# A hybrid mLSTM / RWKV-7 / mixture-of-experts layer on one core: RWKV rows a chunk ahead, output norms as fused pairs, two down pieces behind the product's halves

## Chip, core and metric

The kernel runs on one core of a Trainium2 chip. The metric is the device time of one execution in microseconds (us). The engines are TensorE (PE, with its weight loads PEld), VectorE (DVE), ScalarE (ACT), GpSimd (POOL) and SyncE (SP, which here only issues DMAs).

## What is computed

One layer over 256 context and 2048 latent tokens of width 1024, batch 1, all in float32. Cut to what the change touches:

```python
def _modulate(z, shift, scale):
    return _layernorm(z) * (1 + scale) + shift

    mixed = _mixer(_modulate(ctx, sh1c, sc1c), _modulate(x, sh1, sc1), ...)
    x = _layernorm(ALPHA * x + g1 * (mixed[:, CTX_LEN:] @ w_out[l]), ln1_g[l], ln1_b[l])
    ffn = _hier_moe(_modulate(x, sh2, sc2), ...)
    x = _layernorm(ALPHA * x + g2 * ffn, ln2_g[l], ln2_b[l])

    # in the mixer, RWKV-7, per head, forwards and backwards
    def step(state, inp):
        r_t, w_t, k_t, v_t, kh_t, a_t = inp
        removed = jnp.einsum('zhvk,zhk->zhv', state, kh_t)
        state = (state * w_t[:, :, None, :] - removed[..., None] * (kh_t * a_t)[:, :, None, :]
                 + v_t[..., None] * k_t[:, :, None, :])
        return state, jnp.einsum('zhvk,zhk->zhv', state, r_t)

    # in the experts, 32 of them, top 2 of one group for each token
    hb = jax.nn.silu(xb @ ex_gate[e]) * (xb @ ex_up[e])
    return (hb @ ex_down[e]) * w[:, None]
```

The mixer projects the modulated input, convolves it, runs an mLSTM group and an RWKV-7 group of eight heads each, in both directions, and joins them.

## The kernel before, in words

Stages run one after the other: the input's transpose `make_hT` with the modulation (0 to 125 us), input projection and convolution, token tiles, the mLSTM, RWKV (1241 to 1978 us), the output projection with its two norms (1978 to 2355 us), the experts (2355 to 3520 us) and the last norm. Matrix products that need float32 precision take each operand as a rounded part H and a rest L and add three products, so every operand is split: a cast on ACT or VectorE gives H, a subtraction on VectorE gives L. A scheduler with a model of times sets the order on every engine, except in RWKV, where the program's own order stands for TensorE, VectorE, ACT and SP.

**First stage** (lines 198 to 219). Tokens come in chunks of up to 512. GpSimd issues the loads of four tiles x (line 205), VectorE takes their statistics (lines 75 to 79, the root on ACT) and normalises (line 207). TensorE transposes (line 213), ACT modulates into `hval` (215), VectorE casts to H (218) and subtracts for L (219). The pool of x has five buffers.

**RWKV.** There are nine groups of 256 tokens, each of four chunks of 64, handled for both directions at once (36 chunks). A group needs four builds (two halves, two directions). A build loads `pk` (SP, line 891), takes exponentials (`exps`, ACT, 907 to 909), forms the rows KR and BK (`rows`, VectorE, 919 to 923), multiplies them on TensorE (`products`, 929) with a mask on VectorE into GM (933), and transposes BK into BT (`turn`, 938, 939). A solve inverts a group's triangular matrices by 31 pairs of VectorE operations (`steps`, 978 and 980) on a matrix sM that comes from GM over DRAM; `back` writes the result to DRAM and again into GM, and `join` (1007 to 1024) completes it on TensorE. A chunk itself is a chain between TensorE and ACT or VectorE: start and keys (1051 to 1067), inverse (1076, 1079), update (1086), state (VectorE, 1092 and 1094), outputs (1102, 1105). The next chunk starts from the state S. The main loop (1123 on) calls the chain's parts and puts the builds, the solve's steps and the joins of other groups between them; `PLAN` says which builds belong to which chunk, `CUT` how far the solve has come.

**Output projection** (`project`, from line 1293). For sixteen tiles of 128 tokens: the product on TensorE, the residual on VectorE (1306), then two layer norms in `norm_sums` (1190 to 1201): the mean from sums that earlier passes accumulate, ACT squares (1197) and takes the root (1198), VectorE the reciprocal, and an ACT Identity pass (1201) scales. After it come the gain (1310, VectorE), the bias (1312), the second norm's scale (1315) and shift (1316); 1312 and 1315 run on GpSimd for the first fourteen tiles, on VectorE for the last two. TensorE then transposes the result for the router (1329).

**Experts** (`moe`). Every expert has at least one block of 128 tokens; more blocks run under branches (lines 1710 to 1716). The three weight matrices come through a ring of raw buffers `eraw` and are split into twelve pieces by `split` (1513 cast on ACT, 1514 subtraction on VectorE): 0 to 3 gate, 4 to 7 up, 8 to 11 down. `gate_up` multiplies gate, takes Silu on ACT, multiplies up in two halves of 256 columns; `mult(h)` (1594, VectorE) multiplies a half into `act`, which TensorE transposes (1522) and which is split again (aH 1530, aL 1535) for the down product `epo` in `tail`. `add` scales the output (1623) and adds it to memory.

## Time and profile before

| | us |
|---|---|
| three runs | 3574.02, 3576.32, 3585.05 (median 3576.32) |
| the profiled execution, own time | 3583.68 |
| its span | 3582.1 |
| busy TensorE / weight loads | 2910.9 / 2442.9 |
| busy VectorE / ACT / GpSimd | 2360.3 / 1389.8 / 880.8 |

The mean granted clock of TensorE in it is 0.878 of full speed, and 602.62 MB were moved by DMA, a mean of 168 GB/s. Busy shares over the span (81%, 66%, 39%, 25%) are means over stages with different limits, so the stages have to be looked at one by one. "Idle before, releaser" in a row says how long an engine stood idle just before the instruction, and which event ended that.

### The profile page before, as it was taken

The page shows a single profiled execution, that of the slowest core. Times are in us where ns is not written, and L with a number is a line of the kernel's source. Part 1 is how long each engine was busy: PE and PEld are TensorE (multiplying, and loading weights), DVE is VectorE, ACT ScalarE, POOL GpSimd, SP SyncE. Part 2 cuts the span into 40 slices and gives each one's busy share as a digit, 9 for nine tenths or more (in the row PEclk, how much of TensorE's full clock was granted, in tenths as well). Part 3 has the DMA queues.
Part 4 walks back from the last instruction along what each step waited for, and adds up shares of the span by engine and source line. Part 5 has one row for each costly group of instructions (what it writes and reads, how often), then busy time and mean ns, then how long its engine had stood idle before and what let it go on. Part 6 is the DMA issues. An engine that isn't in the chain of part 4 may idle for free. (4 is left out here: it accounts for less than half of the span.)

```text
span 3582.1 us, 61557 instructions
## 1 busy us (share of the span) xinstructions
PE 2910.9 (81%) x24042; PEld 2442.9 (68%) x24042; DVE 2360.3 (66%) x3863; ACT 1389.8 (39%) x2197; POOL 880.8 (25%) x874
## 2 busy tenths in 40 slices
PE   7999999999889735776666688958888888988892
PEld 4788778987677625665656466757777777877772
DVE  6788888666878745556663677766757545566437
ACT  3432232255453313333333244444535434344223
POOL 1000000024555600111112656531221221221100
PEclk9999999999878756887878799869999999999996
DMA  5333331354685345666663544277978747586535
GB/s 201 119 110 100 120 106 61 104 171 174 203 240 156 119 92 135 148 165 158 154 153 101 177 144 133 93 260 228 314 243 271 254 127 257 161 282 215 175 107 200
DMA packets 471690, 602.62 MB, mean 168 GB/s; under 512 B 127221, under 2 KB 312337, under 8 KB 471313
## 3 DMA queue, kind: packets, MB, share of 16 engines
q1 hardware_dynamic: 413617, 441.15, 39.0%
q0 software_dynamic: 36736, 129.33, 12.9%
q10 hardware_dynamic: 20960, 27.20, 2.3%
q8 instruction: 225, 3.69, 0.4%
q14 instruction: 152, 1.25, 0.1%
HBM read 453.24 MB, written 144.33 MB: 167 GB/s over the span
## 5 line engine op out<-in xcount | busy, mean ns | idle before, releaser
L1514 DVE TENSOR_TENSOR eL<-eraw,eH 128x1024 fp32r<-128x1024 f32 x384 | 443.9, 1218 | 22.1 <-ACT eH L1513 22.1
L329 DVE SCALAR_TENSOR_TENSOR cacc<-P,cw,cacc 128x1008 f32<-128x1008 f32 (+3 forms) x320 | 398.7, 1247 | 54.5 <-ACT cacc L304 44.0
L1513 ACT CAST eH<-eraw 128x1024 fp32r<-128x1024 f32 x384 | 367.8, 1054 | 1.4 <-DVE eL L1514 1.4
L929 PE MATMUL rpg<-KR,BK 64*128 64x128 f32 (+1 forms) x1152 | 121.0, 369 | 211.3 <-DVE KR L923 182.5
L929 PEld LDWEIGHTS rpg<-KR,BK 64*128 64x128 f32 x1152 | 105.0, 267 | 226.7 <-issue 180.5
L263 PE MATMUL in_ps<-hH,w_H 128*128 128x512 f32 (+1 forms) x664 | 251.1, 380 | 1.3 <-ACT pl_ev L355 1.3
L263 PE MATMUL in_ps<-hL,w_H 128*128 128x512 f32 (+1 forms) x664 | 250.2, 377 | 1.0 <-DVE hL L219 1.0
L263 PE MATMUL in_ps<-hH,w_L 128*128 128x512 f32 (+1 forms) x664 | 248.2, 374 | 0.0
L1547 PE MATMUL epo<-eH,aH 128*128 128x512 f32 x408 | 182.3, 447 | 40.0 <-PEq L1710 31.3
L933 DVE TENSOR_TENSOR GM<-rpg,rmask 128x512 f32<-128x512 f32 (+1 forms) x144 | 88.4, 656 | 154.5 <-PE rpg L929 152.3
L1624 POOL DMA_INDIRECT ACC<-yo,ids x32 | 136.7, 4270 | 201.6 <-DVE yo L1623 195.6
L1547 PE MATMUL epo<-eL,aH 128*128 128x512 f32 x408 | 170.2, 417 | 0.0
L1547 PE MATMUL epo<-eH,aL 128*128 128x512 f32 x408 | 163.1, 412 | 0.0
L1564 POOL DMA_INDIRECT xg<-H,ids x48 | 57.6, 1200 | 392.4 <-PE ept L1522 277.6
L1530 ACT CAST aH<-ept 128x256 fp32r<-128x256 f32 x102 | 38.2, 375 | 289.8 <-PE ept L1522 289.8
L1547 PE MATMUL epu<-eL,xH 128*128 128x256 f32 x512 | 148.7, 296 | 0.0
L263 PEld LDWEIGHTS in_ps<-hH,w_H 128*128 128x128 f32 x664 | 125.2, 190 | 34.0 <-issue 10.3
L237 POOL DMA_DIRECT2D w_raw<-in_w_in x28 | 21.2, 757 | 513.4 <-DVE w_L L251 368.9
L1547 PE MATMUL epu<-eH,xL 128*128 128x256 f32 x512 | 146.7, 292 | 0.0
L298 ACT COPY P<-in_ps 128x512 f32<-128x512 f32 (+1 forms) x92 | 51.4, 558 | 239.8 <-PE in_ps L263 239.8
L263 PEld LDWEIGHTS in_ps<-hL,w_H 128*128 128x128 f32 x664 | 125.9, 190 | 24.1 <-issue 2.1
L1547 PE MATMUL epu<-eH,xH 128*128 128x256 f32 x512 | 141.6, 296 | 0.0
(474 smaller groups left out, 8367.0 us busy)
## 6 DMA issues: line engine op xcount, KB each, us to landing
eraw<-in_ex_gate SPq DMA_DIRECT2D x64, 1024.0 KB
eraw<-in_ex_up SPq DMA_DIRECT2D x64, 1024.0 KB
eraw<-in_ex_down SPq DMA_DIRECT2D x64, 1024.0 KB
pk<-PK SPq DMA_DIRECT2D x144, 320.0 KB
PK<-pk POOLq DMA_DIRECT2D x36, 768.0 KB
ada_w<-in_w_ada SPq DMA_DIRECT2D x32, 512.0 KB
v<-MV SPq DMA_DIRECT2D x50, 264.0 KB
kc<-KTd SPq DMA_DIRECT2D x50, 256.0 KB
```

The costliest lines, as they stand in the source:

```text
L237: self.wld = nc.gpsimd.dma_start(w[:, 4:8, o:o + cn], src[:, 4:8])
L263: nc.tensor.matmul(o, a[:, k, :], b, start=i == 0, stop=i == 3 * KT - 1)
L298: nc.scalar.copy(P[:, t0:t0 + n], ps)
L329: nc.vector.scalar_tensor_tensor(o, img[:, r0 + sy:r1 + sy, c0 + sx:c1 + sx], wt(dy, dx), o, op0=OP.mult, op1=OP.add)
L929: nc.tensor.matmul(pG[e][:, q, b.cols], b.BK[HD[e], c, q, :], b.KR[HD[e], c, q, b.cols], start=True, stop=True, tile_position=(64 * e, 0))
L933: nc.vector.tensor_tensor(b.GM[:, c, e::2, b.cols], pG[e][:, :, b.cols], m, op=OP.mult)
L1513: self.cp = nc.scalar.copy(H, w)
L1514: nc.vector.tensor_tensor(L, w, H, op=OP.subtract)
L1530: self.lastc = nc.scalar.copy(A[0][:, ks], ps[:, :step])
L1547: self.pe = nc.tensor.matmul(o, a[:, k, :], b[:, kw, c], start=first and i == 0, stop=last and i == 2)
L1564: return nc.gpsimd.indirect_dma_start(out=x, out_offset=None, in_=self.H2, in_offset=bass.IndirectOffsetOnAxis(ap=ids, axis=0))
L1624: nc.gpsimd.indirect_dma_start(out=self.ACC, out_offset=bass.IndirectOffsetOnAxis(ap=cur[:, 0:1], axis=0), in_=y, in_offset=None, compute_ ...
```

## The change

1. In the first stage, the normalisation of all chunks but the first goes from VectorE to GpSimd, and every second cast to H from VectorE to ACT.
2. In RWKV, all eight builds of the first two groups are made ahead of the first join, each loaded two ahead; in the main loop exponentials and rows of a build come one chunk ahead of its products, loads are issued earlier still, and the solve's steps are cut anew. GM and BT are now allotted with the products; the pool of WC has six buffers.
3. `norm_sums` no longer writes the normalised tile: the two multiply-and-add pairs that follow take mean and reciprocal as per-row operands, two fused VectorE passes for each norm, and the pass over the bias yields the sum for the second norm.
4. In `gate_up` only ten of the twelve pieces are split ahead; the last two behind `mult(0)`. `mult(1)` moves from `tail` to the end of `gate_up`, and two pieces of the next expert are no longer bound behind the last split of this one.

```diff
-                    nc.vector.tensor_scalar(x, x, mu, rs, op0=OP.subtract, op1=OP.mult)
+                    (nc.vector if ci == 0 else nc.gpsimd).tensor_scalar(x, x, mu, rs, op0=OP.subtract, op1=OP.mult)
...
-                    nc.vector.tensor_copy(H, val[:, :n])
+                    (nc.scalar.copy if k % 2 else nc.vector.tensor_copy)(H, val[:, :n])
...
-            CUT = {1: (24, 17), 2: (15, 9), 3: (1, 1)}
+            CUT = [(32, 27, 24), (23, 17, 15), (13, 9, 8), (1, 1, 1)]
...
+                todo = [(n, c2, d) for n in range(2) for c2 in range(2) for d in range(2)]
+                bs = [Build(*a) for a in todo[:2]]
+                for b in bs:
+                    b.exps()
+                    b.rows()
+                for i in range(8):
+                    b = bs[i]
+                    if i + 2 < 8:
+                        bs.append(Build(*todo[i + 2]))
+                    b.products(0)
+                    b.turn(0)
+                    if i + 2 < 8:
+                        bs[i + 2].exps()
+                    b.products(1)
+                    b.turn(1)
+                    if i + 2 < 8:
+                        bs[i + 2].rows()
+                    if i == 3:
+                        old = Solve(0)
...
+                for i in range(36):
+                    n, cc = i // 4, i % 4
+                    k, work, ready = nxt, ready, []
...
+                    if first:
+                        for b in work:
+                            b.products(0)
+                            b.products(1)
+                        if n and n < 8:
+                            z = Solve(n + 1)
+                        old.join(0)
+                    k.start()
+                    k.keys()
+                    if z:
+                        z.steps(CUT[cc][0])
+                        if cc == 3:
+                            z.back()
+                    k.query()
+
+                    more, loads = (loads[:len(plan(i + 1))], loads[len(plan(i + 1)):])
+                    if more:
+                        more[0].exps()
+                    if first:
+                        for b in work[:1]:
+                            b.turn(0)
+                    else:
+                        for b in work:
+                            b.products(0)
+                    if more:
+                        more[0].rows()
+                    k.inverse()
+                    if more[1:]:
+                        more[1].exps()
+                        more[1].rows()
+                    ready = more
...
+                    if z:
+                        z.steps(CUT[cc][1])
+                    k.update()
+                    k.state()
+                    k.outputs()
...
+                    if first:
+                        old.join(1)
+                    if z:
+                        z.steps(CUT[cc][2])
...
-        nc.vector.tensor_tensor(nm, nmu, rs, op=OP.mult)
-        nc.scalar.activation(out, x, AF.Identity, bias=nm, scale=rs)
+        return nmu, rs
...
-                self.norm_sums(tp, x, (sm[:, 0:1], sm[:, 1:2]), "o1", x, t2)
-                nc.vector.scalar_tensor_tensor(x, x, 1.0, l1g, op0=OP.mult, op1=OP.mult, accum_out=sm[:, 2:3])
-                tail = nc.vector if m >= 14 else nc.gpsimd
-                tail.tensor_tensor(x, x, l1b, op=OP.add)
+                nmu, rs = self.norm_sums(tp, x, (sm[:, 0:1], sm[:, 1:2]), "o1", t2)
+                nc.vector.scalar_tensor_tensor(x, x, nmu, l1g, op0=OP.add, op1=OP.mult)
+                nc.vector.scalar_tensor_tensor(x, x, rs, l1b, op0=OP.mult, op1=OP.add, accum_out=sm[:, 2:3])
                 nc.scalar.dma_start(self.ACC[r0], x)
-                self.norm_sums(tp, x, (sm[:, 2:3], sb), "o2", t2, t2, eps2)
-                tail.tensor_tensor(t2, t2, sc2, op=OP.mult)
-                nc.vector.tensor_tensor(t2, t2, sh2, op=OP.add)
+                nmu, rs = self.norm_sums(tp, x, (sm[:, 2:3],), "o2", t2, eps2)
+                nc.vector.scalar_tensor_tensor(t2, x, nmu, sc2, op0=OP.add, op1=OP.mult)
+                nc.vector.scalar_tensor_tensor(t2, t2, rs, sh2, op0=OP.mult, op1=OP.add)
...
+                def more(n, behind):
+                    if R:
+                        with tc.issue_after(behind.ins):
+                            for _ in range(n):
+                                W.append(split(R, len(W)))
...
-                mult(0)
+                m = mult(0)
+                more(2, m)
...
+                mult(1)
...
-                W += [split(Rs[e], i) for i in range(len(W), 12)]
+                W += [split(Rs[e], i) for i in range(len(W), 10)]
...
+                    W = [split(Rs[e + 1], i) for i in range(2)]
                     with tc.issue_after(self.evac[0]), tc.issue_after(self.evac[1]):
-                        W = [split(Rs[e + 1], i) for i in range(AHEAD)]
+                        W += [split(Rs[e + 1], i) for i in range(2, AHEAD)]
```

VectorE, in RWKV where one group's fourth chunk ends and the next group's first chunk runs (S is the state, KR and BK the rows of two builds, GM their masked products, sT and sY a solve's steps); before:

```order
L1094 TENSOR_TENSOR S<-ts,WC 128x512
L919 TENSOR_TENSOR KR_14802<-pk,E_10872 128x4x2x64
L920 TENSOR_TENSOR BK<-pk 128x4x2x64
L921 TENSOR_TENSOR BK<-pk 128x4x2x64
L923 TENSOR_TENSOR KR_14802<-pk,E_10872 128x4x2x64
L919 TENSOR_TENSOR KR_14810<-pk,E_10873 128x4x2x64
L920 TENSOR_TENSOR BK<-pk 128x4x2x64
L921 TENSOR_TENSOR BK<-pk 128x4x2x64
L923 TENSOR_TENSOR KR_14810<-pk,E_10873 128x4x2x64
L933 TENSOR_TENSOR GM_14804<-rpg,rmask 128x4x128 x4
L933 TENSOR_TENSOR GM_14812<-rpg,rmask 128x4x128 x4
L1092 TENSOR_TENSOR ts<-S,rzK 128x512
```

The same place in the changed kernel:

```order
L921 TENSOR_TENSOR KR_14739<-pk,E_10873 128x4x2x64
L935 TENSOR_TENSOR GM_14698<-rpg,rmask 128x4x128 x2
L1087 TENSOR_TENSOR ts<-S,rzK 128x512
L1089 TENSOR_TENSOR S<-ts,WC 128x512
L935 TENSOR_TENSOR GM_14814<-rpg,rmask 128x4x128 x4
L935 TENSOR_TENSOR GM_14840<-rpg,rmask 128x4x128 x4
L973 TENSOR_TENSOR sT<-sM,sY 128x31
L975 TENSOR_TENSOR sY<-sY,sT 128x31
L973 TENSOR_TENSOR sT<-sM,sY 128x60
```

The rows of both builds now end ahead of the fourth chunk's state, and behind the masks stand the first steps of the next solve (five pairs of them, then the chunk's own state update).

VectorE, from the end of one expert to the second half of the next one's product (xL the next tokens' split, aL that of act, ne the branch's count, eL weight pieces, yo the output of the expert before); before:

```order
L1535 TENSOR_TENSOR aL<-ept,aH 128x256
L1661 COPY ne<-blk 1x1
L1662 TENSOR_LOAD ne
L1664 COMPARE_AND_BRANCH
L1664 UNCONDITIONAL_BRANCH x2
L1514 TENSOR_TENSOR eL<-eraw,eH 128x1024 x2
L1623 SCALAR_TENSOR_TENSOR yo<-epo,ids,g2b 128x512
L1514 TENSOR_TENSOR eL<-eraw,eH 128x1024
L1623 SCALAR_TENSOR_TENSOR yo<-epo,ids,g2b 128x512
L1514 TENSOR_TENSOR eL<-eraw,eH 128x1024 x9
L1594 TENSOR_TENSOR act<-act,epu_35414 128x256
L1535 TENSOR_TENSOR aL<-ept,aH 128x256
```

The same place in the changed kernel, from the piece ahead of xL on:

```order
L1532 TENSOR_TENSOR eL<-eraw,eH 128x1024
L1553 TENSOR_TENSOR xL<-epx,xH 128x512 x2
L1553 TENSOR_TENSOR aL<-ept,aH 128x256
L1688 COPY ne<-blk 1x1
L1532 TENSOR_TENSOR eL<-eraw,eH 128x1024
L1689 TENSOR_LOAD ne
L1691 COMPARE_AND_BRANCH
L1691 UNCONDITIONAL_BRANCH x2
L1532 TENSOR_TENSOR eL<-eraw,eH 128x1024 x3
L1650 SCALAR_TENSOR_TENSOR yo<-epo,ids,g2b 128x512
L1532 TENSOR_TENSOR eL<-eraw,eH 128x1024
L1650 SCALAR_TENSOR_TENSOR yo<-epo,ids,g2b 128x512
```

It goes on there with the last three pieces ahead of act, and what follows:

```order
L1532 TENSOR_TENSOR eL<-eraw,eH 128x1024 x3
L1622 TENSOR_TENSOR act<-act,epu_35348 128x256
L1532 TENSOR_TENSOR eL<-eraw,eH 128x1024 x3
L1553 TENSOR_TENSOR aL<-ept,aH 128x256
L1622 TENSOR_TENSOR act<-act,epu_35349 128x256
```

Before, twelve pieces stand ahead of act's first half; now one stands ahead of xL, eight between the count and the first half, and three between that half and aL.

## Rows read from the trace of the kernel before

**Rows 1.** Windows: length, busy PE, PEld, DVE, ACT, POOL, clock, DMA share, GB/s.

```profile
1241.00:1378.00 137.00, 56.78 (x626) 48.36 (x628) 57.18 (x123) 26.54 (x47) 15.72 (x20) 0.54 0.40 96
1378.00:1949.00 571.00, 383.53 (x9082) 340.10 (x9074) 346.86 (x785) 211.52 (x368) 102.61 (x196) 0.79 0.59 149
...
2355.00:3520.00 1165.00, 999.03 (x5516) 871.01 (x5516) 664.59 (x881) 487.93 (x641) 235.29 (x111) 0.92 0.68 216
```

**Rows 2.** Waits of PE, 1452 to 1892 us: total, times, longest.

```profile
PE rpg L929 <- DVE KR L923: 99.9, 18, 6.1
```

**Rows 3.** Timeline of PE: start, duration, engine, line, operation, idle before.

```profile
1713.29 2.08 PE L929 MATMUL rpg<-KR,BK 64*128 64x128 f32 x16 [5.20 <-DVE KR L923]
```

**Rows 4.** Timeline of DVE in RWKV.

```profile
1307.75 1.29 DVE L933 TENSOR_TENSOR GM<-rpg,rmask 128x512 f32<-128x512 f32 x2 [1.72 <-PE rpg L929]
1308.96 0.20 DVE L978 TENSOR_TENSOR sT<-sM,sY 128x31 f32<-128x31 f32 x1
...
1332.10 0.19 DVE L980 TENSOR_TENSOR sY<-sY,sT 128x31 f32<-128x31 f32 x1
1352.33 0.69 DVE L919 TENSOR_TENSOR KR<-pk,E 128x512 f32<-128x512 f32 x1 [20.04 <-ACT E L907]
...
1377.55 0.69 DVE L1094 TENSOR_TENSOR S<-ts,WC 128x512 f32<-128x512 f32 x1
...
1891.77 0.69 DVE L1094 TENSOR_TENSOR S<-ts,WC 128x512 f32<-128x512 f32 x1
...
1948.97 0.69 DVE L1094 TENSOR_TENSOR S<-ts,WC 128x512 f32<-128x512 f32 x1
```

**Rows 5.** Waits of PE in the experts, 2376 to 3393 us.

```profile
PE ept L1522 <- DVE act L1594: 82.4, 29, 3.0
```

**Rows 6.** Timeline of DVE in one expert.

```profile
2700.45 10.30 DVE L1514 TENSOR_TENSOR eL<-eraw,eH 128x1024 fp32r<-128x1024 f32 x9
2710.67 0.41 DVE L1594 TENSOR_TENSOR act<-act,epu 128x256 f32<-128x256 f32 x1
2712.27 0.43 DVE L1535 TENSOR_TENSOR aL<-ept,aH 128x256 fp32r<-128x256 f32 x1 [1.19 <-ACT aH L1530]
```

**Rows 7.** Timeline of PE in the same expert.

```profile
2711.14 0.69 PE L1522 MATMUL ept<-ident,act 128*128 128x128 f32 x2 [2.95 <-DVE act L1594]
...
2714.87 0.40 PE L1547 MATMUL epo<-eH,aL 128*128 128x512 f32 x1
```

**Rows 8.** Windows in the experts.

```profile
2711.10:2714.40 3.30, 2.90 (x13) 2.53 (x14) 0.68 (x2) 0.78 (x2) 0.00 (x0) 0.51 1.05 422
2714.40:2718.00 3.60, 3.60 (x19) 3.04 (x20) 1.82 (x5) 1.76 (x4) 1.00 (x1) 1.00 1.01 392
...
2588.00:2612.00 24.00, 20.76 (x113) 17.85 (x112) 18.35 (x23) 14.41 (x19) 13.88 (x3) 0.93 1.01 358
```

**Rows 9.** Timeline of POOL in the first stage.

```profile
80.37 2.13 POOL L205 DMA_DIRECT2D x<-in_x  x4 [18.15 <-PE hps L213]
100.74 1.61 POOL L205 DMA_DIRECT2D x<-in_x  x3 [18.24 <-PE hps L213]
```

**Rows 10.** Lines 207, 1238 and 812: count, ns min/median/max, first and last start.

```profile
L207 DVE TENSOR_SCALAR x<-x,hx_mv x18: 758/811/815, 19.6 to 111.1; 128x1024 f32<-128x1024 f32 x18
...
L1238 POOL TENSOR_SCALAR ln_g<-ln_g x1: 2796/2796/2796, 1986.5 to 1986.5; 128x1024 f32<-128x1024 f32 x1
...
L812 POOL TENSOR_SCALAR pk<-pk,cv,kb x36: 548/555/2603, 725.2 to 994.5; 128x256 f32<-128x256 f32 x36
```

**Rows 11.** Timeline of DVE in the first stage.

```profile
92.99 0.81 DVE L207 TENSOR_SCALAR x<-x,hx_mv 128x1024 f32<-128x1024 f32 x1
```

**Rows 12.** Waits of DVE, 1241 to 1978 us.

```profile
DVE sT L978 <- DMA sM<-BL: 54.8, 8, 7.9
```

**Rows 13.** Lines 1201, 1312 and 1315 in the output projection.

```profile
L1201 ACT ACTIVATE x<-x,o_ns x16: 1227/1242/1246, 2050.8 to 2332.7; 128x1024 f32<-128x1024 f32 x16
...
L1312 POOL TENSOR_TENSOR x<-x,ln_b x14: 2339/2390/3372, 2056.2 to 2305.8; 128x1024 f32<-128x1024 f32 x14
...
L1315 POOL TENSOR_TENSOR t<-t,sc2b x14: 2349/2374/2446, 2064.8 to 2316.9; 128x1024 f32<-128x1024 f32 x14
```

**Rows 14.** Timeline of DVE in the output projection.

```profile
2052.06 1.23 DVE L1310 SCALAR_TENSOR_TENSOR x<-x,ln_g 128x1024 f32<-128x1024 f32 x1 [1.18 <-ACT x L1201]
...
2055.07 2.23 DVE L1310 SCALAR_TENSOR_TENSOR x<-x,ln_g 128x1024 f32<-128x1024 f32 x1
```

**Rows 15.** Timeline of POOL in the output projection.

```profile
2054.95 1.27 POOL L1276 TENSOR_TENSOR mix<-yy 128x512 f32<-128x512 f32 x1 [5.13 <-PE opt L1288]
```

**Rows 16.** Groups by line in the experts: busy us, mean ns.

```profile
L1514 DVE TENSOR_TENSOR eL<-eraw,eH 128x1024 fp32r<-128x1024 f32 x348 | 402.4, 1218 | 21.2 <-ACT eH L1513 21.2
```

**Rows 17.** Timeline of DVE, starts of two experts of one block.

```profile
2746.11 0.13 DVE L1661 COPY ne<-blk 1x1 int32<-1x1 int32 x1
...
2769.15 0.13 DVE L1661 COPY ne<-blk 1x1 int32<-1x1 int32 x1
```

More of the change, by code (lines that the diff above doesn't have):

```diff
@@ L904, in exps @@
                     if b.d == 0:
[L905 removed]
+                        wcs[b.n, b.c2] = gp.tile([128, 2, 4, 2], F, name="WC", bufs=6)
                     b.WC = wcs[b.n, b.c2]
@@ L939, in turn @@
                     nc.scalar.copy(b.BT[:, c], pT)
-                def all(b):
-                    b.exps()
-                    b.rows()
-                    for c in range(2):
-                        b.products(c)
-                        b.turn(c)
             GMf = lambda n, c2, d: G[n, c2, d][2].rearrange("p c h t -> p (c h) t")
@@ L1182, in load_rows, with norm_sums @@
         return t
-    def norm_rows(self, pool, x, tag, out=None):
+    def norm_sums(self, pool, x, sums, tag, sq, eps=None):
         nc = self.nc
-        mu, rs = self.ln_stats(pool, x, D, LN_EPS, tag)
-        nm = pool.tile([128, 1], F, name=tag + "_nm")
-        nc.vector.scalar_tensor_tensor(nm, mu, -1.0, rs, op0=OP.mult, op1=OP.mult)
-        nc.scalar.activation(x if out is None else out, x, AF.Identity, bias=nm, scale=rs)
-    def norm_sums(self, pool, x, sums, tag, out, sq, eps=None):
-        nc = self.nc
-        st = pool.tile([128, 4], F, name=tag + "_ns")
-        nmu, v, rs, nm = (st[:, i:i + 1] for i in range(4))
-        nc.vector.tensor_scalar(nmu, sums[0], sums[1], -1.0 / D, op0=OP.add, op1=OP.mult)
+        st = pool.tile([128, 3], F, name=tag + "_ns")
+        nmu, v, rs = (st[:, i:i + 1] for i in range(3))
+        if len(sums) == 2:
+            nc.vector.tensor_scalar(nmu, sums[0], sums[1], -1.0 / D, op0=OP.add, op1=OP.mult)
+        else:
+            nc.vector.tensor_scalar(nmu, sums[0], -1.0 / D, None, op0=OP.mult)
         nc.scalar.activation(sq, x, AF.Square, bias=nmu, accum_out=v)
```

100 lines of the change are left out of this document (33 added, 67 removed).

## Prediction, made before the result was known

> **What bounds the kernel now.** I read the busy time by stage first [rows 1]. In the RWKV chunks (1378 to 1949 us) neither TensorE (383.53 of 571 us) nor VectorE (346.86) is full, and the granted clock is 0.79: the stage is a chain of waits, and so is the preamble ahead of it (56.78 and 57.18 us of 137). In the experts (2355 to 3520 us) TensorE is busy 999.03 of 1165 us, VectorE 664.59, the DMA share is 0.68. Then I asked, stage by stage, which wait ends last on TensorE.
>
> In RWKV it waits for the rows KR: 99.9 us in a stretch of 440 us, 18 times, at most 6.1 us [rows 2]. [Rows 3] shows one: sixteen products start 5.20 us late, because VectorE built the rows only behind its steps of the solve. Groups of four chunks follow one another: state updates at 1377.55 and 1891.77 us enclose seven of them [rows 4], so one takes 73.5 us. In the experts TensorE's largest wait is for the product "act": 82.4 us, 29 times [rows 5]; [rows 6, 7] show one. Nine pieces "eL" stand in one row on VectorE, 10.30 us, the product of 0.41 us stands behind them, and the transposes start 2.95 us late. [Rows 8] shows what follows: in the 3.30 us behind that wait the clock is 0.51, the lower level (1.2 GHz); in the next 3.60 us it is 1.00.
>
> **First stage.** A chunk of 512 columns is one serial loop: its loads are issued at 80.37 us, the next ones at 100.74 [rows 9], because five x buffers serve four tiles per chunk. The change puts the four normalisations of a chunk on GpSimd. On VectorE one takes 811 ns [rows 10]; the last of the chunk starts at 92.99 us [rows 11] and ends at 93.80. GpSimd has no such instruction in the trace. The nearest rows are its tensor_scalar of 128x256, 555 ns (four times as wide: 2.2 us), and one of the same shape with other operands, 2.80 us [rows 10]. Four in a row from about 87.4 us (statistics run closer together without normalisations between) end at 96.2 to 98.6 us, 2.4 to 4.8 us later. I take 3.2, nearer the first, which has the same two per-row operands. Three chunks one after the other make +10 us. The half of the casts that moves to ACT hides beside VectorE's subtractions; without that cover it would cost what it saves. Bounds: -3, if VectorE's relief sets the loop, to +20, if the longer price also delays the next loads, which stand behind the normalisations in GpSimd's queue.
>
> **RWKV.** Preamble: the builds ahead of the solve fill VectorE up to 1308.96 us, from 1241, and the solve ends at 1332.10; then VectorE waits 20.04 us for the exponentials of two builds whose loads stood behind the solve's, and the first state comes 25.2 us behind that [rows 4]. Now all eight builds come first, the loads two ahead, and nothing is loaded between solve and join. The 20 us go; of the 68 us before the solve I take off 15, since a build's own work on VectorE is four row products of 0.69 and four masks of 0.65 (5.4 us, [rows 4]) and the rest of its 11 us is waiting that a neighbour now fills. One comes back in the join: -34, from -20 (the wait alone) to -45.
>
> Groups: of 73.5 us, 99.9/6 = 16.6 are waits for KR [rows 2]. With the rows a chunk ahead these end, and three waits are late next. In a group's first chunk the solve's first steps stand on VectorE ahead of the state, and their matrix arrives 54.8/8 = 6.9 us after the last mask [rows 12]. In the second the exponentials stand on ACT behind the chunk's copies, the rows behind them, so VectorE idles some 4 us (my layout of the order). In the fourth the second build's rows need a BK buffer (the pool has two), free only after the other build's second turn: some 3 us. Of the 16.6 I keep 7.9: seven groups give -55. The eighth, 57.2 us from 1891.77 to 1948.97 [rows 4], gets the same, -8. RWKV in sum -97, from -60 to -130 (all 16.6 in seven groups would be -116 by itself).
>
> **Output projection.** Per tile of 128 tokens two ACT passes of 1.24 us go, and GpSimd's two of 2.39 and 2.37; VectorE does four wide passes where it did two, each 1.23 us [rows 13, 14], so it gets 2.5 us more work in a step of 19 us (fourteen tiles between 2056.2 and 2305.8 us, [rows 13]). The chain of one tile becomes some 5 us shorter, but tiles overlap. What surely lies on the path is the last two tiles, where VectorE did GpSimd's part already: two ACT and two narrow VectorE operations less, near 3 us; the rest is a part of TensorE's stalls behind such chains. I take -10, from -25 to +8.
>
> A row speaks against it: the VectorE pass that took 1.23 us at 2052.06 took 2.23 at 2055.07 [rows 14], while a GpSimd pass ran from 2054.95 for 1.27 us [rows 15]. One such hold per tile is +16, and the stage would be +6. I keep -10, because GpSimd loses two passes per tile and so most of its chances to collide. The Trainium skill, "SBUF — State Buffer", section "Who interferes with whom", says that a VectorE instruction with two SBUF inputs takes its second input through a port that GpSimd's reads use too, and that whoever comes first holds the shared ports for the whole instruction. By that rule the stage would be the +6; the trace agrees with its mechanism (1.00 us longer).
>
> **Experts.** Before, all pieces stand ahead of the product's first half; now one moves ahead of the next tokens' split, where VectorE idled, and three go behind the first half. Four fewer at 10.30/9 = 1.14 us [rows 6] or 1.22 us [rows 16] are 4.6 to 4.9 us, more than the wait of 2.95. So the wait goes, and of the 3.30 us at half clock some 1.6. New is a wait on VectorE: the split aL of act ended 1.6 us after the product [rows 6], and ends 3 x 1.14 + 0.43 = 3.9 us after it now. TensorE came to the matmul that reads it 3.8 us after the product, at 2714.87 [rows 7]; without the low clock it comes after some 2.5, and waits 1.35 us. Per expert -2.95 - 1.6 + 1.35 = -3.2 us, on 23.04 us (starts at 2746.11 and 2769.15, [rows 17]). Thirty-one times: -99. The weight stream holds back some of it: a window with one block per expert already has a DMA share of 1.01 at 358 GB/s [rows 8]; in experts of more blocks it is slack, and a ring of raw buffers carries some of that over. I take 9 off: -90, from -50 to -125 (no late aL).
>
> **Sum.** +10 - 97 - 10 - 90 = -187. The profiled execution's own time is 3583.7 us, so it would come to 3396.7; the median of the runs shown is 3576.3, 7.4 lower, and gives 3389.
>
> **Rivals.**
> 1. The weight stream or the late aL takes half of the experts' gain. For it: share 1.01 at 358 GB/s [rows 8]; against it, the stage's mean of 0.68 [rows 1]. The experts give -45: 3434.
> 2. The RWKV group hardly falls, since the waits for exponentials, BK and the matrix take what KR's wait gave. For it: the waits of 6.9 us [rows 12]; against it, VectorE's 346.86 busy of 571 us [rows 1]. Only preamble and last group stay, -42 instead of -97: 3444. With rival 1: 3489.
> 3. Slower: the pieces behind the product hold the last raw weight buffer longer, its next load is issued later, and TensorE meets missing weights in every expert. It decides from the point where every expert ends 187/31 = 6.0 us later than forecast; with 8 us the time is 3389 + 31 x 8 = 3637. Against it: [rows 5] shows that act is what is waited for, and the buffer is held only some 4 us longer.
> 4. The change does not do what it says: the three pieces could still be put ahead of the product. The order of instructions shows them behind, so 1 in 50, and then the experts give nothing: 3479.
>
> **How the numbers follow.** Forecast 0.6, rival 1 0.16, rival 2 0.13, both 0.05, rival 3 0.03, rival 4 0.02, and 0.01 for other things. The predicted time is the likeliest, 3389. The four terms' bounds (about 12, 35, 17 and 38 us each way) add in squares to 56, so its own range is 3333 to 3445. Rivals 1 and 2 lie in it or at its end; I go to 3460 for their own spread, and to 3325 below. About 0.3% (11 us) is what a measurement can tell from no change: faster by more 0.95, within it 0.02, slower 0.03.
>
> **What would show it.** First stage: loads 23 to 24 us apart instead of 20.4. RWKV: no wait of TensorE for KR over 1 us in the groups, first states of groups 65 to 66 us apart, the first of all near 1342 us plus what the first stage adds. Output projection: steps below 19 us. Experts: no wait of the transposes for act, a new one of the down matmul for aL near 1.35 us, one-block experts 19.5 to 20.5 us apart, the clock above 0.9 behind the product. I am wrong if one-block experts stay above 22 us, or groups above 70.

## The result, and the profile after

The changed kernel takes 3422.95 us (median; 3418.58 to 3430.39), the kernel before 3580.69 in the same comparison. The ratio is 0.9563, with a 95% interval of 0.9538 to 0.9588: 4.4% faster, 157.7 us. The forecast was 187 us less, 3389 in a range of 3325 to 3460.

The two profiled executions differ by 165.1 us in span (3582.1 and 3417.0). Split at the last subtraction of the first stage (line 219), the first exponential of RWKV, the first and the last state update, the first count `ne` of the experts and their last output, they differ as follows; times are those of the timeline's rows.

| stretch | before | after | difference | forecast |
|---|---|---|---|---|
| start to the end of the first stage | 123.6 | 140.2 | +16.6 | +10 |
| from there to RWKV's first exponential | 1108.2 | 1107.9 | -0.3 | 0 |
| RWKV, to the first state | 146.4 | 128.2 | -18.2 | -34 |
| RWKV, first to last state | 600.1 | 568.1 | -32.0 | -63 |
| last state to the experts' first count | 400.9 | 361.2 | -39.7 | -10 |
| experts | 1138.3 | 1046.6 | -91.7 | -90 |
| last norm | 64.5 | 64.8 | +0.3 | 0 |

So the sum was near because errors of both signs met. The windows of the changed kernel, from RWKV's preamble on (length, busy PE, PEld, DVE, ACT, POOL, clock, DMA share, GB/s):

```profile
1248.00:1376.00 128.00, 57.46 (x640) 48.84 (x641) 66.12 (x146) 30.23 (x56) 25.88 (x39) 0.57 0.53 128
1376.00:1944.00 568.00, 421.78 (x9761) 376.18 (x9762) 350.56 (x781) 223.71 (x387) 108.87 (x212) 0.81 0.61 154
1944.00:2305.00 361.00, 275.94 (x1334) 216.80 (x1334) 289.26 (x673) 128.09 (x231) 178.03 (x128) 0.87 0.48 156
2305.00:3352.00 1047.00, 952.82 (x5506) 830.16 (x5506) 648.19 (x853) 476.21 (x628) 217.97 (x101) 0.98 0.74 239
```

The last three of these stretches in the kernel before:

```profile
1378.00:1978.00 600.00, 404.31 (x9786) 358.83 (x9778) 351.33 (x791) 222.81 (x388) 109.43 (x212) 0.80 0.58 146
1978.00:2379.00 401.00, 295.89 (x1335) 234.37 (x1335) 293.94 (x680) 163.95 (x261) 236.30 (x156) 0.82 0.43 145
2379.00:3518.00 1139.00, 996.37 (x5504) 868.91 (x5503) 647.26 (x851) 476.27 (x628) 220.81 (x102) 0.93 0.69 219
```

The preamble of RWKV still has TensorE busy for 57 of 128 us, as little as before [rows 1]. The chunks lost 32 us while VectorE's busy time stayed (351.33 before, 350.56 now): idle time went, no work. (The 383.53 and 346.86 us of [rows 1] end at 1949 us, one group before the last state, and cannot be set beside these.) In the output projection the granted clock rose from 0.82 to 0.87, and VectorE's busy time did not grow (293.94 before, 289.26 now). In the experts TensorE does the same products in 952.82 us of busy time instead of 996.37, at a clock of 0.98 instead of 0.93: little is left of the stretches at half clock behind the waits [rows 8].

**First stage.** The line view of the normalisation, then GpSimd's timeline:

```profile
L207 POOL TENSOR_SCALAR x<-x,hx_mv x16: 3769/3772/4267, 20.7 to 127.0; 128x1024 f32<-128x1024 f32 x16
```

```profile
86.42 2.16 POOL L205 DMA_DIRECT2D x<-in_x  x4 [2.87 <-PE hps L213]
93.48 15.06 POOL L207 TENSOR_SCALAR x<-x,hx_mv 128x1024 f32<-128x1024 f32 x4 [4.90 <-DVE hx_mv L79]
112.64 1.65 POOL L205 DMA_DIRECT2D x<-in_x  x3 [4.10 <-PE hps L213]
```

One pass takes 3.77 us, above both bounds of the prediction (2.2 and 2.80). Four take 15.06 us in a row, and loads are now 26.2 us apart instead of 20.4 [rows 9].

**RWKV.** VectorE's timeline in the changed kernel: the first solve's first step, the first state; rows, steps and state of one second chunk; rows and state of the fourth chunk of the same group; then the state seven groups behind the first.

```profile
1325.84 0.20 DVE L973 TENSOR_TENSOR sT<-sM,sY 128x31 f32<-128x31 f32 x1
...
1375.54 0.69 DVE L1089 TENSOR_TENSOR S<-ts,WC 128x512 f32<-128x512 f32 x1
...
1588.96 0.69 DVE L917 TENSOR_TENSOR KR<-pk,E 128x512 f32<-128x512 f32 x1 [5.32 <-ACT E L907]
...
1591.43 0.38 DVE L973 TENSOR_TENSOR sT<-sM,sY 128x220 f32<-128x220 f32 x1
...
1596.29 0.42 DVE L975 TENSOR_TENSOR sY<-sY,sT 128x255 f32<-128x255 f32 x1
1596.64 0.68 DVE L1087 TENSOR_TENSOR ts<-S,rzK 128x512 f32<-128x512 f32 x1
...
1627.11 0.69 DVE L918 TENSOR_TENSOR BK<-pk 128x512 f32<-128x512 f32 x1 [2.98 <-PE rpg L940]
...
1630.12 0.68 DVE L1087 TENSOR_TENSOR ts<-S,rzK 128x512 f32<-128x512 f32 x1
...
1863.27 0.69 DVE L1089 TENSOR_TENSOR S<-ts,WC 128x512 f32<-128x512 f32 x1
```

Seven groups take 487.7 us, 69.7 each instead of 73.5 [rows 4]; the forecast was 65.6. TensorE's wait for KR [rows 2] is gone, and its waits are now for the state. TensorE's timeline around that second chunk's update, then in an expert of one block:

```profile
1591.20 1.15 PE L1081 MATMUL rzK<-UV,BT 128*64 128x64 f32 x32 [1.31 <-ACT UV L1074]
...
1598.10 1.13 PE L1046 MATMUL rzK<-S,KR 64*64 64x64 f32 x32 [4.81 <-DVE S L1089]
...
2651.70 0.38 PE L1540 MATMUL ept<-ident,act 128*128 128x128 f32 x2
...
2655.58 0.47 PE L1565 MATMUL epo<-eH,aH 128*128 128x512 f32 x1 [2.35 <-DVEq L1737]
```

The update ends at 1592.35; the state could follow, but VectorE begins it at 1596.64, behind six pairs of the solve's steps (1591.43 to 1596.71). Before the rows VectorE had stood idle for 5.32 us. VectorE's waits, 1380 to 1860 us (total, times, longest):

```profile
DVE KR L917 <- ACT E L907: 54.7, 14, 8.6
DVE sT L973 <- DMA sM<-BL: 48.0, 7, 8.4
...
DVE BK L918 <- PE rpg L940: 6.5, 3, 3.0
```

**Experts.** In TensorE's rows above the transposes of act wait no longer; the down product waits 2.35 us. VectorE in the same expert, with the counts of two experts ahead of it:

```profile
2618.40 0.13 DVE L1688 COPY ne<-blk 1x1 int32<-1x1 int32 x1
...
2639.09 0.13 DVE L1688 COPY ne<-blk 1x1 int32<-1x1 int32 x1
...
2650.89 0.42 DVE L1622 TENSOR_TENSOR act<-act,epu 128x256 f32<-128x256 f32 x1 [1.03 <-PE epu L1565]
2651.23 3.49 DVE L1532 TENSOR_TENSOR eL<-eraw,eH 128x1024 fp32r<-128x1024 f32 x3
2654.63 0.42 DVE L1553 TENSOR_TENSOR aL<-ept,aH 128x256 fp32r<-128x256 f32 x1
```

An expert of one block takes 20.69 us instead of 23.04 [rows 17]. VectorE now idles 1.03 us ahead of the product where it was late before [rows 6], and the split aL ends 3.74 us behind it. TensorE's waits in this stage, 2328 to 3273 us (line 1737 is the branch for an expert's further blocks, where TensorE waits until VectorE has reached it):

```profile
PE epo L1565 <- DVEq L1737: 28.2, 12, 2.4
...
PE epo L1565 <- DVE aL L1553: 10.7, 11, 1.0
```

The output projection's lines stand with their experiment below.

### The profile page after: what moved, and what is told of

It reads as the page before. It is cut to its first block, busy times and chain, and to the rows that moved or that the text cites. A ratio compares the mean times of both kernels' runs of the same rounds, so it can differ in the third digit from the quotient of the medians.

```text
span 3417.0 us, 61401 instructions
## 1 busy us (share of the span) xinstructions
PE 2866.9 (84%) x24042; PEld 2405.9 (70%) x24042; DVE 2339.6 (68%) x3822; ACT 1364.0 (40%) x2187; POOL 879.0 (26%) x862
## 5 line engine op out<-in xcount | busy, mean ns | idle before, releaser
L1531 ACT CAST eH<-eraw 128x1024 fp32r<-128x1024 f32 x384 | 370.9, 1052 | 48.3 <-PEq L1737 35.1
L1565 PE MATMUL epo<-eH,aH 128*128 128x512 f32 x408 | 172.2, 422 | 64.8 <-DVEq L1737 32.2
L1565 PE MATMUL epo<-eL,aH 128*128 128x512 f32 x408 | 163.2, 400 | 0.0
L931 PE MATMUL rpg<-KR,BK 64*128 64x128 f32 (+1 forms) x1152 | 122.4, 350 | 46.7 <-ACT BT L941 17.5
L973 DVE TENSOR_TENSOR sT<-sM,sY 128x31 f32<-128x31 f32 (+15 forms) x279 | 95.3, 342 | 78.8 <-DMA sM<-BL 70.8
L263 PEld LDWEIGHTS in_ps<-hH,w_L 128*128 128x128 f32 x664 | 126.1, 190 | 22.3 <-issue 0.8
L1565 PEld LDWEIGHTS epo<-eH,aH 128*128 128x128 f32 x408 | 78.9, 193 | 83.1 <-ACT xH L1548 30.7
```

Source lines behind the costliest of these rows:

```text
L263: nc.tensor.matmul(o, a[:, k, :], b, start=i == 0, stop=i == 3 * KT - 1)
L931: nc.tensor.matmul(pG[e][:, q, b.cols], b.BK[HD[e], c, q, :], b.KR[HD[e], c, q, b.cols], start=True, stop=True, tile_position=(64 * e, 0))
L973: nc.vector.tensor_tensor(tt, M[:, 0:j, j:j + 1].to_broadcast([128, j, w]), Y[:, j:j + 1, j:32].to_broadcast([128, j, w]), op=OP.mult)
L1531: self.cp = nc.scalar.copy(H, w)
L1565: self.pe = nc.tensor.matmul(o, a[:, k, :], b[:, kw, c], start=first and i == 0, stop=last and i == 2)
```

## Experiments

All runs are of the changed kernel with the edit that is shown. Ratios are to the kernel before, measured beside it; the changed kernel's own is 0.9563.

**Normalisations back on VectorE.**

```diff
-                    (nc.vector if ci == 0 else nc.gpsimd).tensor_scalar(x, x, mu, rs, op0=OP.subtract, op1=OP.mult)
+                    nc.vector.tensor_scalar(x, x, mu, rs, op0=OP.subtract, op1=OP.mult)
```

> The changed kernel with the first stage's normalisations back on VectorE; every second cast stays on ACT. Theory: the whole loss of the first stage is GpSimd's pass of 3.77 us, four in a row per chunk; the last subtraction of the stage then ends at 121 to 126 us instead of 140.2, and the time is 3400 to 3410 us against 3423. Rival: the casts on ACT (0.62 us against 0.43) lengthen the modulation's queue as well; then the stage ends at 130 us or later and the time is 3413 to 3420.

3407.30 us, ratio 0.9514 (0.9487 to 0.9542). The end of the stage in VectorE's timeline:

```profile
121.83 0.68 DVE L219 TENSOR_TENSOR hl<-hval,hl 128x512 fp32r<-128x512 f32 x1
```

It ends at 122.5 us, 17.6 earlier than with GpSimd and 1.1 earlier than before the change. GpSimd's pass is the whole loss; sharing the casts with ACT costs nothing, and a gain is not shown (in the four runs with the normalisations on VectorE the stage ends between 121.6 and 125.0 us).

**Norms as before, but none on GpSimd.** Four VectorE passes and the two ACT Identity passes:

```diff
-                nmu, rs = self.norm_sums(tp, x, (sm[:, 0:1], sm[:, 1:2]), "o1", t2)
-                nc.vector.scalar_tensor_tensor(x, x, nmu, l1g, op0=OP.add, op1=OP.mult)
-                nc.vector.scalar_tensor_tensor(x, x, rs, l1b, op0=OP.mult, op1=OP.add, accum_out=sm[:, 2:3])
+                self.norm_sums(tp, x, (sm[:, 0:1], sm[:, 1:2]), "o1", x, t2)
+                nc.vector.scalar_tensor_tensor(x, x, 1.0, l1g, op0=OP.mult, op1=OP.mult, accum_out=sm[:, 2:3])
+                nc.vector.tensor_tensor(x, x, l1b, op=OP.add)
...
```

> The changed kernel with the output projection's norms as before (ACT Identity pass, then gain, bias, scale, shift as four VectorE passes), but none of them on GpSimd. Theory: the gain of 40 us in this stage is GpSimd's two slow passes leaving the chain and its ports; with them on VectorE the stage from the last RWKV state to the first expert's count stays within 8 us of 361, and the time within 3418 to 3432. Rival: the shorter chain by fused pairs (no ACT Identity passes) brings most of it; then the stage is 15 to 35 us longer and the time 3438 to 3458.

3439.36 us, ratio 0.9609 (0.9585 to 0.9633). The stage, from 1939 to 2316 us in its window:

```profile
1939.00:2316.00 377.00, 280.32 (x1331) 218.75 (x1331) 292.78 (x704) 165.11 (x262) 170.59 (x128) 0.87 0.47 150
```

It takes 377.2 us from the last state to the first count, between the 361.2 of the fused pairs and the 400.9 before. So of the 39.7 us, 23.7 come from taking GpSimd's two passes out and 16.0 from the fused pairs, which drop the two ACT passes. Neither theory was whole; the rival's lower bound is met. What the 23.7 us are is not settled. GpSimd's passes were long links in a tile's chain, but VectorE operations that no edit touched also became shorter when they went, such as line 746 (min/median/max in ns), before and in this run:

```profile
L746 DVE TENSOR_SCALAR rh_st<-rh_st x16: 156/517/1856, 2008.0 to 2292.1; 128x8 f32<-128x8 f32 x16
```

```profile
L746 DVE TENSOR_SCALAR rh_st<-rh_st x16: 160/168/1216, 1965.9 to 2226.4; 128x8 f32<-128x8 f32 x16
```

The granted clock of the stage is 0.87 here too, as in the changed kernel, against 0.82 before. The run does not tell these three apart.

**All twelve pieces ahead of the product.**

```diff
-                more(2, m)
...
-                W += [split(Rs[e], i) for i in range(len(W), 10)]
+                W += [split(Rs[e], i) for i in range(len(W), 12)]
```

> The changed kernel with all twelve pieces split ahead of the product's first half again; the second half's product stays ahead of the branch, and one piece stays ahead of the next tokens' split. Theory: VectorE's whole queue up to the branch sets an expert, wherever the pieces stand in it, so one-block experts stay at 20.3 to 21.3 us and the time is between 3413 and 3445 us; what moved the experts from 23.2 was the second half's product ahead of the branch and the early piece. Rival, the prediction's reason: the product's wait behind the pieces is what counts, and one-block experts go back to 22.5 to 23.3 us, the time to 3480 to 3505.

3448.94 us, ratio 0.9645 (0.9620 to 0.9669). In VectorE's order no piece stands behind the product now. Experts of one block take 21.6 us, between the theories; the stage takes 1076.4 us. TensorE waits for act again, but less than in [rows 5]; the window of the stage stands below the wait:

```profile
PE ept L1540 <- DVE act L1621: 51.8, 29, 1.9
```

```profile
2304.80:3381.20 1076.40, 958.63 (x5503) 830.34 (x5503) 647.20 (x851) 476.28 (x628) 335.95 (x101) 0.97 0.72 232
```

The pieces behind the product are thus worth 29.8 us of the stage's 91.7. The other 61.9 come with what this kernel keeps: the piece ahead of the next tokens' split, and the second half's product ahead of the branch. The clock is 0.97 here, against 0.93 before and 0.98 in the changed kernel: most of the half clock ends with these two edits, though TensorE still waits for act 29 times, up to 1.9 us, and not with the pieces behind the product.

**The second half's product back behind the branch.**

```diff
                 with behind():
                     for k in range(6, 8):
                         up(k, 1)
-                mult(1)
...
             def tail(W, fill, mid=None):
+                mult(1)
```

> The changed kernel with the second half's product back behind the branch; the pieces stay behind the first half. Theory: the product ahead of the branch is what took the rest of the experts' gain, since TensorE waits at the branch; one-block experts take 21.3 to 22.5 us instead of 20.6, those of 24.7 to 25.8 us about 28 again, and the time is 3440 to 3475. Rival: the early piece ahead of the next tokens' split brought that rest; then the product's place is worth under 0.3 us per expert and the time stays within 3415 to 3432.

3421.90 us, ratio 0.9554 (0.9521 to 0.9587), one-block experts mostly 20.7 us: the place of this product is worth nothing while the pieces stand behind the first half. TensorE's wait at the down product is nearly the same, 30.3 us in 15 times here:

```profile
PE epo L1565 <- DVEq L1737: 30.3, 15, 2.0
```

By this the early piece would hold the rest of the gain, but it was not undone alone, nor was the product's place with all pieces ahead.

**Eleven pieces ahead.**

```diff
-                more(2, m)
+                more(1, m)
...
-                W += [split(Rs[e], i) for i in range(len(W), 10)]
+                W += [split(Rs[e], i) for i in range(len(W), 11)]
```

> The changed kernel with eleven pieces named ahead of the product's first half and one behind it (two stand behind it in VectorE's order, where three did). Theory: VectorE idles 1.0 us before the first half's product, and the branch waits 2.3 us for the split aL behind three pieces; one piece moved forward fills the first and shortens the second, so one-block experts take 19.4 to 20.1 us and the time is 3388 to 3410. Rival: the weights' split as a whole or the DMA share of 0.9 to 1.0 holds the expert at 20.6, or the product becomes late again as with all twelve ahead: 3418 to 3440.

3388.70 us, ratio 0.9468 (0.9437 to 0.9499). VectorE in two experts:

```profile
2624.42 0.13 DVE L1688 COPY ne<-blk 1x1 int32<-1x1 int32 x1
...
2636.25 0.42 DVE L1622 TENSOR_TENSOR act<-act,epu 128x256 f32<-128x256 f32 x1
2636.58 2.36 DVE L1532 TENSOR_TENSOR eL<-eraw,eH 128x1024 fp32r<-128x1024 f32 x2
2638.85 0.42 DVE L1553 TENSOR_TENSOR aL<-ept,aH 128x256 fp32r<-128x256 f32 x1
...
2643.95 0.13 DVE L1688 COPY ne<-blk 1x1 int32<-1x1 int32 x1
```

19.53 us per expert, and the product starts without idle time ahead of it. One piece moved from behind the product to ahead of it gains 1.1 us per expert, about one piece. The DMA share in a window of two of these experts is 1.04 at 364 GB/s:

```profile
2605.00:2644.00 39.00, 35.21 (x210) 30.55 (x209) 34.15 (x41) 25.83 (x33) 13.43 (x4) 1.00 1.04 364
```

The raw weights are read by ACT's casts and VectorE's subtractions, and neither waits for a load in it, so the stream was not the bound at 23, nor at 20.7, nor is it shown to be at 19.5.

**The solve's steps cut anew.**

```diff
-            CUT = [(32, 27, 24), (23, 17, 15), (13, 9, 8), (1, 1, 1)]
+            CUT = [(32, 27, 24), (17, 17, 15), (11, 11, 8), (1, 1, 1)]
```

> The changed kernel with the solve's steps cut anew: in a group's second chunk all steps stand ahead of the new rows and none between rows and state, in the third two more ahead of the masks and none between. Theory: steps of the solve that stand on VectorE between rows and state hold up the state by 4 us in the second chunk and 2 to 3 in the third, while VectorE idles for 5 and 2 us before the rows; the period falls from about 70 to 63 to 66 us, the time by 25 to 45 us to 3378 to 3398. Rival: the steps fill time in which the chain waits for TensorE anyway; the period stays above 68 us and the time within 10 us of 3423.

3390.75 us, ratio 0.9472 (0.9451 to 0.9494). The states of a third, fourth, first and second chunk in VectorE's timeline:

```profile
1597.62 0.69 DVE L1089 TENSOR_TENSOR S<-ts,WC 128x512 f32<-128x512 f32 x1
...
1617.58 0.69 DVE L1089 TENSOR_TENSOR S<-ts,WC 128x512 f32<-128x512 f32 x1
...
1635.76 0.69 DVE L1089 TENSOR_TENSOR S<-ts,WC 128x512 f32<-128x512 f32 x1
...
1651.93 0.69 DVE L1089 TENSOR_TENSOR S<-ts,WC 128x512 f32<-128x512 f32 x1
```

The second chunk takes 16.2 us here (14 to 18 over the run, 16 to 21 in the changed kernel), the third 11.4 (14.3 to 15.5 in the changed kernel), the fourth 20.0 (16 to 18 there): steps that no longer delay the third meet the fourth, and part of the gain is handed on. Seven groups fell from 487.7 to 458.0 us. The theory holds.

**A third BK buffer.**

```diff
-                    b.BK = wp.tile([128, 2, 4, 128], F, name="BK")
+                    b.BK = wp.tile([128, 2, 4, 128], F, name="BK", bufs=3)
```

> The changed kernel with three BK buffers instead of two. Theory: in a group's fourth chunk the second build's rows wait some 3 us for a BK buffer that the other build's second turn frees, and the chunk's state stands on VectorE behind them; with a third buffer the period of a group falls by 2 to 4 us, the time by 14 to 30 us to 3393 to 3409. Rival: the chunk's chain (sYT copy and exponentials on ACT ahead of the inverse's copy) ends as late; the period stays within 1 us, the time within 3416 to 3430.

3409.66 us, ratio 0.9527 (0.9496 to 0.9557). The fourth chunk falls to 15.3 us and the group by 3.2 us on average (seven take 465.5 us, 22.2 less), and the view of VectorE's waits lists none for BK any more. The wait of 2.98 us above is the late wait that the prediction named, at its price in the groups. The time fell by 13.3 us only, which ends 0.7 us above the theory's range, and the ratio's interval still meets the changed kernel's; the buffer's worth is read from the groups. One place gave time back: in this trace the stretch from the last state to the experts' first count takes 368.0 us instead of 361.2. In all five runs with the new cut or the third buffer it takes 366.9 to 370.9 us, in the others that leave this stage alone 362.1 to 364.5; no run shows why.

**The first solve between the builds**, and the same with the eighth build's load first:

```diff
                     b = bs[i]
+                    if i == 5:
+                        old.steps(1)
+                        old.back()
                     if i + 2 < 8:
                         bs.append(Build(*todo[i + 2]))
...
-                old.steps(1)
-                old.back()
```

> The changed kernel with the first solve's steps and its way back put ahead of the sixth build's products instead of behind the eighth's. Theory: the first solve's matrix is there at about 1306 us, 20 us before its steps begin, because all eight builds' operations stand ahead of them on VectorE; now the steps begin by 1314, the last three builds fill the way over DRAM, and the first state comes 7 to 15 us earlier: 3408 to 3416. Rival: VectorE has as much to do up to the join in either order (the loads set the pace), and the first state moves by less than 3 us: 3418 to 3428.

3424.27 us, ratio 0.9561 (0.9528 to 0.9593): nothing; the first state comes at 1379.66 us, later than the changed kernel's 1375.54. The solve did end early, as ACT's timeline shows, whose copy sYT follows its last step, but the last build's exponentials came late:

```profile
1336.59 1.97 ACT L980 COPY sYT<-sY 128x1024 f32<-128x1024 f32 x1 [24.68 <-DVE sY L975]
...
1355.24 0.63 ACT L907 ACTIVATE E<-pk 128x512 f32<-128x512 f32 x1 [16.20 <-DMA pk<-PK]
```

On SP's queue the eighth load stood behind the way back, whose first DMA was issued at 1336.58 us:

```profile
1347.58 2.19 SPq L891 DMA_DIRECT2D pk<-PK  x4
```

In the second run the three added lines stand behind `bs.append`.

> As the run that put the first solve ahead of the sixth build's products, but with the eighth build's load issued ahead of the solve's way back on SP's queue. Theory: there the solve ended 13 us earlier and the first state still came late, because that load stood on SP behind the way back's DMAs (issued at 1347.6 us, exponentials at 1355.2); issued first, the first state comes 10 to 18 us earlier than in the changed kernel, 1358 to 1366 us, and the time is 3405 to 3414. Rival: the masks and products of the last three builds and TensorE at half clock fill that time, and it stays within 4 us: 3419 to 3427.

3407.28 us, ratio 0.9515 (0.9493 to 0.9536). The exponentials come at 1337.48 us, the first state's update at 1361.67 instead of 1375.54; counted from RWKV's first exponential, which differs by 1.4 us, that is 115.0 instead of 127.5. So the first of the two runs failed because its edit had put the way back ahead of a load on the same queue, and the second shows what the solve's place is worth: 12.5 us of the preamble. (Its seven groups take 477.3 us instead of 487.7 as well; why is not shown.)

**Together.** Four edits: normalisations, new cut, third buffer, eleven pieces.

> The changed kernel with four edits of these runs together: normalisations on VectorE, the steps cut anew, three BK buffers, eleven pieces ahead. Theory: they act in different stages or chunks, so their differences of 15.6, 32, 13 and 34 us add: 3315 to 3345. Rival: the new cut and the third buffer act on the same fourth chunk, and half of one is lost, and the weight stream holds the experts when they start earlier: 3346 to 3365.

3314.26 us, ratio 0.9253 (0.9233 to 0.9274), 108.7 us under the changed kernel's median, where the four differences make 95: they add, and more. The surplus stands in the groups: seven take 422.4 us, 65.3 less than in the changed kernel, where the new cut alone gave 29.7 and the third buffer alone 22.2. The fourth chunk, to which the cut alone had handed a wait (20.0 us), takes 17.0 with both. Two more edits, the first solve as in the last run and the way back behind the inverse:

```diff
-                        if cc == 3:
-                            z.back()
...
                     ready = more
+                    if cc == 3 and z:
+                        z.back()
```

> The four edits together, the first solve between the builds with the load first, and the solve's way back behind the fourth chunk's inverse instead of ahead of it. Theory: the transposing copy of 2 us and the exponentials stand on ACT ahead of the inverse's copy, which comes 3.9 us after its products in the run with the new cut; behind it the fourth chunk loses 2 to 4 us in each group, and the preamble 10 to 15: 3285 to 3318. Rival: the later way back makes the next join wait, and only the preamble gains: 3318 to 3332.

3309.55 us, ratio 0.9233 (0.9214 to 0.9253). The fourth chunk fell from 17.0 to 15.1 us, the first chunk of the next group rose from about 17.5 to 20.7 to 24.1. VectorE's wait for the next solve's matrix, 1400 to 1860 us, here and then with four edits:

```profile
DVE sT L973 <- DMA sM<-BL: 86.4, 7, 15.1
```

```profile
DVE sT L973 <- DMA sM<-BL: 58.8, 7, 9.7
```

The last run takes the way back's move out again.

> The run of six edits without the later way back: the solve's way back stands again ahead of the fourth chunk's inverse. Theory: with six edits the fourth chunk fell from 17.0 to 15.1 us, and the next group's first chunk rose from 17 to 18 to 21 to 24, because the join then waits for the way back and the next matrix comes later; ahead of the inverse the period is 58 to 62 us as with four edits, and the preamble's 10 us stay: 3298 to 3308. Rival: the first chunk rose for the preamble's reordering, not for the way back; then the period stays near 61.5 and the time at 3308 to 3316.

3304.32 us, ratio 0.9244 (0.9215 to 0.9272). The chunks are 17.0 and 16 to 19 us again, but seven groups take 430.9 us, against 429.3 with the move: where the way back stands moves time between two chunks and takes none away. With the four edits alone the groups took 422.4, but the stretch from the first exponential to the first state 124.7 us where it is 112.0 now: what the preamble gains the groups lose in part. The period of 61.6 us fits theory and rival, the time only the theory. The intervals of the last three runs overlap; that five edits beat four is not shown, that each beats both kernels is.

## Why the prediction was right, and where it was not

In the table's stages with a forecast the errors are +6.6, +15.8, +31.0, -29.7 and -1.7 us. That the largest two nearly cancel is luck.

**First stage: right in kind, too small.** The serial loop grew as the prediction said, with the next loads behind it. The term that was mis-sized is the price of GpSimd's pass: taken near 2.2 us from the 128x256 row, it measures 3.77. In the prediction's sum that price would have made 8.7 us per chunk; 2.8 of them came back, because the next loads follow the last pass by 4.10 us now and followed it by 6.94 before (from 93.80 to 100.74 us). The loop grew by 5.8 us instead of 3.2, three times 5.8 is 17.4, and the stage lost 16.6.

**RWKV's preamble: half.** The 20.04 us between solve and join went: the step that failed is "of the 68 us before the solve I take off 15". The 68 us were counted from 1241 us; from RWKV's first exponential the stretch was 77.1 us, and it is 77.8 now (the steps begin at 1325.84 us), since all eight builds stand ahead of them on VectorE, where six did. SP and ACT in the changed kernel:

```profile
1300.27 1.77 SPq L965 DMA_DIRECT2D sM<-BL  x2
```

```profile
1309.99 0.63 ACT L907 ACTIVATE E<-pk 128x512 f32<-128x512 f32 x1 [6.82 <-DMA pk<-PK]
```

The solve's matrix was on its way at 1300 to 1302 us. Two more builds cost what the overlap gained. The run with the load first recovers 12.5 us, near the 15 that were wrongly taken off, but in another way: its steps begin 65.1 us behind the first exponential because they no longer stand behind the last three builds.

**RWKV's groups: right in kind, half in size.** The wait for KR went, and the three late waits that were named came about as written: the matrix 48.0/7 = 6.9 us, BK up to 2.98 us (run: -22 us in seven groups), the second chunk's exponentials 5.32 us in the row shown (4 was taken). What failed is "of the 16.6 I keep 7.9": 3.8 was kept. The layout let the state follow the chain's update and missed that steps of the solve stand between rows and state on VectorE: 4.3 us in the second chunk (1592.35 to 1596.64), and again in the third. The new cut showed it: -32 us of the time. Rival 2 (the group hardly falls) was half true, through a wait that it did not name. The prediction's sign of being wrong, groups above 70 us, was just missed by the mean of 69.7; the seven run from 65.5 to 71.8, and four of them are above 70. The eighth group gave -7.8, as forecast (-8); the last three chunks, which the forecast left out, grew by 2.3.

**Output projection: wrong in size by four.** The step that failed is "tiles overlap ... the rest is a part of TensorE's stalls"; the -39.7 us lie outside its bounds of -25 to +8. A step took 16.6 us (line 1329 below: sixteen starts from 2013.1 to 2262.5) instead of 19. The prediction counted 2.5 us more work for VectorE in a step; in sum none came, since other operations on it became shorter or went. What set the step before were GpSimd's two slow passes, worth 23.7 us by the run without them (as links of the chain, by holding VectorE up, or by TensorE's clock, which is not settled), and the ACT passes, worth 16.0. The rise of the granted clock from 0.82 to 0.87 stands in no term of the prediction. The row that spoke against it did come back, but did not set the sign. The fused passes in the changed kernel:

```profile
L1329 DVE SCALAR_TENSOR_TENSOR x<-x,o_ns,ln_g x16: 1261/1286/2324, 2013.1 to 2262.5; 128x1024 f32<-128x1024 f32 x16
```

The longest of sixteen is 2.32 us, as long as the one held up before [rows 14], the median 1.29. Of the 64 fused passes in the stage's four lines 15 took over 1.5 us, together some 10 us more than at the median, and each of the 15 began while a GpSimd pass was under way; one such hold per tile would have been 16 us. By the rule of the Trainium skill, "SBUF — State Buffer", section "Who interferes with whom", that a VectorE instruction with two SBUF inputs contends with a GpSimd instruction that reads SBUF, the prediction would have had the stage 6 us longer; passes of this length are in the trace, but the stage became 39.7 us shorter.

**Experts: right in sum, one step off in mechanism.** The wait for act went, and most of the half clock, and the late aL took its place as said: 2.35 us for the down product in the row shown, where 1.35 was forecast. It shows as VectorE's branch and not as aL itself; with the product behind the branch the wait is nearly the same, so it is VectorE's queue behind the pieces. Of the fall, 29.8 us hang on the pieces behind the product and 61.9 on two other edits: the second half's product, which the prediction did not price, and the early piece, which it counted as one of four. The step off is the clock: the prediction let the half clock end with the wait for act, but with all twelve pieces ahead that wait stayed at up to 1.9 us and the clock was at 0.97 all the same. Which of the two edits brings how much of the 61.9 is open; the run with the second half's product moved back speaks for the early piece. The 9 us taken off for the weight stream were not lost to it; the down product's longer wait, 1 us more in each of 12, is of that size. Rival 1, the weight stream, is refuted: at 19.5 us per expert still no cast or subtraction waited for a weight's load. Rival 3 did not occur for the same reason, and rival 4 is out by the timeline, where the three pieces stand behind the product.

## What to carry to other kernels

When operations move from one place of an engine's order to another, lay out what then stands ahead of each operation that the next chain step waits for, and fill the engine's idle time before it moves work behind: two pieces behind the product were better than three and better than none, and solve steps in front of the wait were better than behind it. An operation that is put ahead of a load on the same queue holds that load up; one run lost its whole gain to that. A slow engine can set a step even where its busy share is low, and the way to see it is to put the same operations on a faster engine; whether it does so by its place in the chain or by holding up others is then still to be asked.

## What the runs showed of the hardware that was not expected

GpSimd's tensor_scalar with two per-row operands took 3.77 us for 128x1024, 6.8 times the 555 ns of 128x256 and a third more than the 2.80 us of the same shape at line 1238; VectorE needs 0.81 us. The DMA engines carried 364 GB/s at a share of 1.04 over 39 us of experts without ACT or VectorE waiting for a weight's load, so a share of about 1 did not mean that the stream was late.
